# Two-layer RWKV-7 and differential-attention step: another deal of pair 9's matmuls, earlier loads in pair 0, and a group of outputs turned by VectorE and DMA

## Chip, cores and metric

The kernel runs on one core of a Trainium2 chip. The time is device microseconds from start to end of one execution; it is taken several times, and the median counts. The engines are TensorE (PE; its weight loads are shown apart as PEld), VectorE (DVE), ScalarE (ACT), GpSimd (POOL) and SyncE (SP), which issues nearly all DMAs. Each works through its own queue in order, and semaphores make one wait for another.

## What is computed

A trunk of two layers runs over 512 prompt tokens and 32 sample tokens. Each layer has one input projection, a token mixer, four heads of attention over a memory of 256 rows, a SiLU gate and one output projection.

```python
def rwkv_layer(...):           # layer 0
    h = rmsnorm(x, norm_w)
    p, qm, gate = jnp.split(h @ w_in, [RW_PROJ, RW_PROJ + MEM_W], axis=-1)
    y_mix, S_T, last_row = rwkv_mixer(p, ...)      # 24 heads of 64, a state update for each token
    y_mem = mem_attention(qm, mk, mv)
    out = jnp.concatenate([y_mix.astype(x.dtype), y_mem], axis=-1) * jax.nn.silu(gate)
    return x + out @ w_out, S_T, last_row

def diff_layer(...):           # layer 1
    attn = probs(q1, k1) - lam * probs(q2, k2)     # 12 heads, masked by chunks of 64
    o = einsum('bhqk,bkhd->bqhd', attn, v_all)
    o = rmsnorm(o, subln) * (1.0 - lam_init)
    out = jnp.concatenate([o, y_mem], axis=-1) * jax.nn.silu(gate)
    return x + out @ w_out, k, v
```

The memory's keys and values, the mixer's last state, and layer 1's keys and values are outputs as well.

## The kernel before

All large products are made of matmuls of 128x128 weights by 272 tokens, each operand split into a high and a low part, three matmuls a product (`ps_g<-hh,whi`, `hl,whi`, `hh,wlo`). They are the filling of the program: a stream hands out one at a time, and everything else is placed between them. A block of 48 such matmuls makes 128 columns of a projection; its weights come by DMA as `raw` and are split by ACT (`whi`) and DVE or POOL (`wlo`) one block ahead.

**Layer 0** does the 24 mixer heads as 12 pairs. For a pair `pr` the loop at L1540 runs through `PLAN`, 23 steps of two halves. At each step it issues one piece of the pair's chain over eight chunks of tokens (`go("chain", pr)`, three steps a chunk), then the plan's pieces of later pairs: `prep` two pairs ahead, which ends with the pair's chunk matrices in `at` and stores their diagonal blocks to DRAM (`sc<-at`, step 11, first half); `inv`, which loads them in another layout (`m<-sc`) and inverts them on POOL; `back`, which stores the inverse (`sc<-u`, step 9); `at` (L802), five DMAs that load it into `at` (`at<-sc`, `ats<-sc`, step 11, second half); and `mrg`, which from step 16 puts the inverse together with 32x32 matmuls, the first of which reads a DVE transpose of it (`t1b`, `ps_w<-t1b,at`). After each half it hands out filling matmuls until the planned time `t` reaches the half's due time. `each[pr]` counts the pair's filling matmuls: 130 for pair 0, 192 for pairs 1 to 8, 10 and 11, and 144 for pair 9. Due times (L1546) are spread over the steps by `pace` (L1545): evenly, or by each step's DVE load where the pair has fewer than 144. The DMAs go out on SP in program order, and one that waits holds up all behind it.

**Layer 1** is one stream of 2688 positions, a position being one filling matmul. Each of the 12 heads has three blocks (values, keys, queries), gates, and for heads 1, 3, 5 and 7 the query and gate of a memory head; head 5, the sixth, starts at position 1152 and has 288. Work is set on positions relative to a head's start `f`: at 52 the values are turned and later stored, at 99 and 108 the keys are split, exchanged by DMA (`kh<-kh`) and stored (`scr<-sg`); scores come at 156, 188, 220 and 254 (`ps_s`, then exponentials on ACT), and the normalized weights of each tile are turned by DVE in 32x32 blocks into `pk`. At 304 `pk` is stored by four DMAs (`ptr<-pk`), at 360 loaded back as `aT`, and at 440 multiplied with the values (`ps_o`), with the result scaled into `ot`. Four heads are a group.

At the end of a group, `norms` (L2080) makes the norm of its outputs, `scaled` (L2085) applies it to one head's `ot` and `finished` (L2099) turns it so that the model dimension lies on the partitions and multiplies it by the gate. There are two ways to turn it, chosen by `OTURN`, the number of groups that go the second way. In the first, four PE transposes write `ps_oT`. In the second, `spread` (L1792) transposes 32x32 blocks on DVE into `to` and four DMAs put the blocks of 128-byte rows in their places in DRAM (`spread<-to`); a DMA loads the result (`turned_back`). `to` has one buffer, which the memory heads' probabilities (`mspread<-to`) and the cached keys (`to<-ck`) use too. With `OTURN = 0` all three groups go the first way. The first group's norms stand at `begin(5) + NORM1` and its `finished` at positions 106, 130, 154 and 178 of head 5.

A memory head of layer 1 (`mem_steps`, L1134) is a generator of 14 pieces, set on positions by `MEMAT1`, for the last one, in head 7, by `MEMAT1B`: loads, scores and weights of two tiles each, three turns by `spread` (pieces 8, 11 and 12), the loads of the turned weights (13), and the product with the values (14, `ps_mo`). Head 8 starts 240 positions after head 7.

Of the kernel before, what the change touches and what calls it, by code (L numbers as in the profile page):

```python
# [19 lines left out]
KT = D // P  # L20
# [17 lines left out]
MEM1 = (1, 3, 5, 7)  # L38
TILES1 = ((156,178),(188,210),(220,244),(254,280))
MEMAT1 = (60, 80, 180, 276, 294, 306, 324, 330, 346, 362, 402, 420, 484, 552)  # L40
MEMAT1B = MEMAT1[:10] + (400, 430, 490, 590)
LOADS1, SPLITS1 = (1, 26), (4, 10, 14, 20)
SAMPLE1 = ((310, "s"), (338, "m"), (362, "t"), (386, "w"), (406, "n"), (464, "r"))
SAMPLE2 = ((186, "s"), (214, "m"), (228, "t"), (264, "w"), (311, "n"), (336, "r"))
TILES2 = ((152, 180), (210, 236), (240, 268), (272, 304))
BACK1, SUMS1, NORM1 = 80, 160, 52
BACK2, SUMS2, NORM2 = 54, 112, 34
SUMS3 = 22
NORM1B = 76
OTURN = 0  # L50
MTURN = True
CTURN = True
STEP, GAP1, GAP2 = 60, 70, 112
LATE = (186, 222, 254, 290)
OUT1 = 24
RKV = 4
# [13 lines left out]
PLAN = [  # L70
    [[("val", 0, 0.95, 0), ("prep", 2, 0.1, 0)], [("prep", 2, 0, 0.42)]],
    [[], [("prep", 2, 0, 1.04)]],
    [[("prep", 1, 0.53, 0)], [("prep", 1, 0, 0), ("prep", 2, 0.56, 1.0)]],
    [[("prep", 2, 0, 0)], [("prep", 2, 0, 1.0)]],
    [[("smp", 0, 0.11, 0.28), ("prep", 1, 0.4, 0)], [("prep", 2, 0, 0.86)]],
    [[("out", -1, 0.11, 0)], [("prep", 2, 0, 0.84)]],
    [[("prep", 2, 0, 1.1), ("smp", 0, 0.21, 0.29)], [("prep", 2, 0, 0.86)]],
    [[("prep", 2, 1.1, 1.37)], []],
# [52 lines left out]
class Trunk:  # L131
# [1219 lines left out]
    def layer0(self, mem):  # L1351
# [6 lines left out]
        with ExitStack() as ctx:  # L1358
# [24 lines left out]
            def go(kind, pr):  # L1383

                if kind == "rsq":
                    self.rsqrt(self.r20[:], self.q20[:], self.rk0, "nt20")
                elif 0 <= pr < NPAIR:
                    if kind in ("inv", "back", "at"):
                        {"inv": self.rw_invert, "back": self.rw_back, "at": self.rw_at}[kind](sts[pr])
                        return  # L1390
                    if (kind, pr) not in run:
                        it = run[kind, pr] = self.rw_prep(sts[pr], rkv[pr]) if kind == "prep" else make[kind](sts[pr])
                        next(it)
                    next(run[kind, pr], None)


            blocks, each = [], [0] * NPAIR
# [95 lines left out]
            def shift_out():  # L1493

                ps = self.psm.tile([P, 512], F32, tag="m", name="ps_sh")
                so = self.ma.tile([NPROJ, 2, P], F32, name="sho")
                for q in range(2):
                    self.te.transpose(ps[:NPROJ, q * P : q * P + P], self.shc[:, q, :], self.ident[:])
                self.ae.copy(so[:], ps[:NPROJ, :256].rearrange("p (q c) -> p q c", q=2))
                for q, n in ((0, 3), (1, 9)):  # L1500
                    self.se.dma_start(o[n][0, 0].rearrange("(j p) -> j p", p=P), so[:, q, :])
# [37 lines left out]
            for pr in range(NPAIR):  # L1539
                mplan = MPLAN.get(pr, ())  # L1540
                took = [HOP + sum(us for x in y for kind, d, us, _ in x if 0 <= pr + d < NPAIR) for y in PLAN]
                load = [HOPV[k % 3] + sum(us for x in y for kind, d, _, us in x if 0 <= pr + d < NPAIR) for k, y in enumerate(PLAN)]
                whole = sum(took) + MEMPE * len(mplan) / 12 + MAIN * each[pr]

                pace = [max(x, 1.4) for x in load] if each[pr] < 3 * 6 * KT else [1.0] * len(PLAN)  # L1545
                due = [whole * sum(pace[:k]) / sum(pace) for k in range(len(PLAN) + 1)]  # L1546
                room = (sum(load) + 2.3 * each[pr] / 48) / len(PLAN)
                t, left, spent = 0.0, each[pr], 0.0
                for k, y in enumerate(PLAN):
                    go("chain", pr)  # L1550
                    t += HOP
                    if (pr, k) == SHIFT_OUT:
                        shift_out()
                    spent += HOPV[k % 3]
                    for half, x in enumerate(y):
                        for kind, d, us, vus in x:
                            if 0 <= pr + d < NPAIR and kind != "full":
                                go(kind, pr + d)
                                t += us
                                spent += vus  # L1560
                        for at, h in mplan:
                            if at == k + half / 2:
                                if h not in mit:
                                    mit[h] = self.mem_steps(mems[h], 0, h, self.ma)
                                    next(mit[h])
                                next(mit[h], None)
                                t += MEMPE / 12
                        if k + half / 2 in EPLAN.get(pr, ()):
                            next(early)
                        if FULL not in x:  # L1570
                            spent += self.some(room * (k + (half + 1) / 2) + 0.4 - spent)
                        while left and t + MAIN / 2 < (due[k + 1] if half else (due[k] + due[k + 1]) / 2):
                            next(main)
                            t += MAIN
                            left -= 1
                while left:
                    next(main)
                    left -= 1
                if pr + 3 == NPAIR:
                    for _ in range(3):  # L1580
                        go("prep", pr + 2)
                    while self.later:
                        self.later.pop(0)[0]()
                    ca.close()
                    early = self.early_tiles(self.pool("wo0e", 1, ctx=mctx, side="right"), made)
                    self.ma = self.pool("mem0a", 1, ctx=ma, side="right")
# [10 lines left out]
        with ExitStack() as ctx:  # L1597
# [49 lines left out]
            pr = [self.psc.tile([P, 512], F32, tag="c", name="ps_r") for _ in range(2)]  # L1647
# [169 lines left out]
    def diff_layer(self, dq, p, mp, mctx, pool_early, order, made):  # L1817
# [7 lines left out]
        def at(pos, fn):  # L1825
            ev.append((pos, len(ev), fn))
# [45 lines left out]
        def make_query(ms):  # L1872
            def make(w):
                ms["q"], evac = self.query_evac(mp)
                yield from self.steps(w, lambda ps, v: evac(ps, v) and None)
            return make

        def make_mem_gate(ms, m):
            def make(w):
                _, ms["gate"], evac = self.gate_evac(self.o1[12 + m])  # L1880
                yield from self.steps(w, evac)
            return make
# [202 lines left out]
        def scaled(G, j):  # L2085
            ot = G["on"][j]
            self.ve.tensor_tensor(ot[:], ot[:], G["ss"][:, 2, 4 * j : 4 * j + 4].unsqueeze(2).to_broadcast([P, 4, P]), ALU.mult)
# [11 lines left out]
        def finished(G, hg, j):  # L2099
            if hg < OTURN:  # L2100
                x = G.pop(("oT", j))[:].rearrange("p t q -> p (t q)")
            else:
                ps = self.psm.tile([P, 512], F32, tag="m", name="ps_oT")
                for t in range(4):
                    self.te.transpose(ps[:, t * P : t * P + P], G["on"][j][:, t, :], self.ident[:])
                x = ps[:]
            g = self.o1[4 * hg + j]
            self.ve.scalar_tensor_tensor(g[:, :TP], x, self.subs, g[:, :TP], ALU.mult, ALU.mult)
            self.ve.tensor_tensor(g[:, TP:], G["oT"][:, 32 * j : 32 * j + 32], g[:, TP:], ALU.mult)
# [12 lines left out]
        for h, st in enumerate(sts):  # L2122
# [24 lines left out]
            if h in MEM1:  # L2147
                m = MEM1.index(h)
                makes += [make_query(mems[m]), make_mem_gate(mems[m], m)]
                for off in MEMAT1B if h == MEM1[-1] else MEMAT1:  # L2150
                    at(f + off, lambda m=m: next(mits[m], None))
            if h % 4 == 3:
# [5 lines left out]
                for j in range(4):  # L2158
                    if hg >= OTURN and not last:
                        at(b + 18 + 14 * j, lambda G=G, j=j: scaled(G, j))  # L2160
# [131 lines left out]
```

## Time and profile before

| | |
|---|---|
| median of 3 runs | 1372.35 us (1371.68 to 1373.49) |
| the profiled execution | 1371.31 us, of which 1369.6 us are span |
| mean granted TensorE clock | 0.991 |
| layer 0's pairs, first chain piece of each | 140 to 598 us, about 45.6 us apart |
| layer 1's stream | 826 to about 1260 us |

Rows of the timeline have the start and the length in us, the engine (SPq is SP's DMA queue), the operation, what it writes and reads (out<-in), its shape and its count, and in brackets how long the engine was idle before it and what released it. Rows of the waits have the engine and what it writes, what it waited for, and the sum, the number and the longest of these waits. A window's row has its stretch and length, the busy us and instructions of PE, PEld, DVE, ACT and POOL, the granted clock, the share of the DMA engines and GB/s.

### The profile page before, as it was taken

The page shows a single profiled execution, that of the slowest core. Times are in us where ns is not written, and L with a number is a line of the kernel's source. Part 1 is how long each engine was busy: PE and PEld are TensorE (multiplying, and loading weights), DVE is VectorE, ACT ScalarE, POOL GpSimd, SP SyncE. Part 2 cuts the span into 40 slices and gives each one's busy share as a digit, 9 for nine tenths or more (in the row PEclk, how much of TensorE's full clock was granted, in tenths as well). Part 3 has the DMA queues.
Part 4 walks back from the last instruction along what each step waited for, and adds up shares of the span by engine and source line. Part 5 has one row for each costly group of instructions (what it writes and reads, how often), then busy time and mean ns, then how long its engine had stood idle before and what let it go on. Part 6 is the DMA issues. An engine that isn't in the chain of part 4 may idle for free. (4 is left out here: it accounts for less than half of the span.)

```text
span 1369.6 us, 31286 instructions
## 1 busy us (share of the span) xinstructions
PE 1324.5 (97%) x11600; PEld 1268.7 (93%) x11600; DVE 888.7 (65%) x2203; ACT 771.8 (56%) x2090; POOL 562.0 (41%) x986
## 2 busy tenths in 40 slices
PE   6999999999999999999999999999999999999997
PEld 6998899999999999888899999999999999999997
DVE  6766667877787778756673374545675556767443
ACT  6665767677767776655652354545444454554321
POOL 1317675568556855560130034444333343542000
PEclk9999999999999999999999999999999999999998
DMA  7643223322332233233364456767676758784721
GB/s 230 185 118 76 62 67 86 86 74 63 86 86 74 63 86 77 74 84 99 99 206 128 133 154 180 179 143 181 143 174 146 171 134 179 169 190 145 241 70 66
DMA packets 418291, 171.47 MB, mean 125 GB/s; under 512 B 195210, under 2 KB 402579, under 8 KB 418139
## 3 DMA queue, kind: packets, MB, share of 16 engines
q1 hardware_dynamic: 417994, 168.96, 47.7%
q8 instruction: 91, 1.49, 0.5%
q14 instruction: 62, 0.50, 0.1%
q10 hardware_dynamic: 144, 0.52, 0.1%
HBM read 130.84 MB, written 41.92 MB: 126 GB/s over the span
## 5 line engine op out<-in xcount | busy, mean ns | idle before, releaser
L128 PE MATMUL ps_g<-hl,whi 128*128 128x272 f32 x1872 | 544.9, 294 | 0.6 <-POOL hl L500 0.5
L128 PE MATMUL ps_g<-hh,wlo 128*128 128x272 f32 x1808 | 538.7, 298 | 1.3 <-DVE wlo L128 1.3
L128 PE MATMUL ps_g<-hh,whi 128*128 128x272 f32 x1808 | 537.4, 297 | 0.9 <-ACT hh L128 0.9
L128 PEld LDWEIGHTS ps_g<-hl,whi 128*128 128x128 f32 x1872 | 353.7, 190 | 2.8 <-POOL hl L500 0.7
L128 PEld LDWEIGHTS ps_g<-hh,whi 128*128 128x128 f32 x1808 | 344.3, 190 | 5.3 <-ACT hh L128 1.3
L128 PEld LDWEIGHTS ps_g<-hh,wlo 128*128 128x128 f32 x1808 | 343.7, 190 | 5.8 <-DVE wlo L128 2.1
L128 ACT CAST whi<-raw 128x512 fp32r<-128x512 f32 x322 | 190.8, 617 | 95.1 <-PE ps_g L128 51.0
L789 POOL TENSOR_TENSOR tm<-u,m 102x84 f32<-102x84 f32 (+23 forms) x372 | 156.7, 421 | 165.8 <-DMA m<-sc 137.8
L338 POOL TENSOR_TENSOR wlo<-raw,whi 128x512 fp32r<-128x512 f32 x110 | 142.0, 1308 | 185.3 <-ACT whi L128 166.7
L128 DVE TENSOR_TENSOR wlo<-raw,whi 128x512 fp32r<-128x512 f32 x212 | 153.5, 739 | 74.5 <-ACT whi L128 73.1
L791 POOL TENSOR_TENSOR u<-u,tm 102x84 f32<-102x84 f32 (+23 forms) x372 | 159.0, 427 | 29.1
L128 PE MATMUL ps_g<-lo,whi 128*128 128x272 f32 x448 | 129.5, 289 | 0.7 <-DVE lo L128 0.7
L128 PE MATMUL ps_g<-hi,wlo 128*128 128x272 f32 x448 | 129.5, 289 | 0.2 <-DVE wlo L128 0.2
L128 PE MATMUL ps_g<-hi,whi 128*128 128x272 f32 x448 | 129.5, 289 | 0.1
L128 PEld LDWEIGHTS ps_g<-lo,whi 128*128 128x128 f32 x448 | 84.4, 188 | 1.1 <-DVE lo L128 1.1
L128 PEld LDWEIGHTS ps_g<-hi,wlo 128*128 128x128 f32 x448 | 84.5, 189 | 0.4 <-DVE wlo L128 0.4
L128 PEld LDWEIGHTS ps_g<-hi,whi 128*128 128x128 f32 x448 | 84.5, 189 | 0.3 <-ACT whi L128 0.3
L128 DVE SCALAR_TENSOR_TENSOR SB<-ps_c,dl,sd 64x64 f32<-64x64 f32 x168 | 47.3, 282 | 43.5 <-PE ps_c L128 39.3
L128 ACT COPY sv<-ps_c 64x64 f32<-64x64 f32 x192 | 39.2, 204 | 38.9 <-PE ps_c L128 37.1
L1890 POOL TENSOR_TENSOR kz<-k,kh 64x544 fp32r<-64x544 f32 x24 | 33.4, 1392 | 53.3 <-ACT kh L128 52.4
L1660 POOL TENSOR_TENSOR hl<-hn,hh 128x544 fp32r<-128x544 f32 x8 | 12.4, 1557 | 92.6 <-ACT hh L128 92.5
L128 ACT ACTIVATE qp<-ps_g 64x272 fp32r<-64x272 f32 x48 | 18.8, 391 | 50.6 <-DVE qp L128 33.7
(395 smaller groups left out, 2560.9 us busy)
## 6 DMA issues: line engine op xcount, KB each, us to landing
raw<-in_rw_in_dram SPq DMA_DIRECT2D x114, 256.0 KB
raw<-in_df_in_dram SPq DMA_DIRECT2D x112, 256.0 KB
raw<-in_w_out_dram SPq DMA_DIRECT2D x64, 256.0 KB
ptr<-pk SPq DMA_DIRECT2D x44, 160.0 KB
aT<-ptr SPq DMA_DIRECT2D x11, 640.0 KB
scr<-sg SPq DMA_DIRECT2D x96, 68.0 KB
out_dram<-scr SPq DMA_DIRECT2D x6, 1024.0 KB
m<-sc SPq DMA_DIRECT2D x36, 128.0 KB
```

Of the source, the lines that this page charges most:

```text
L128: return lambda *a, **k: self.trunk.tie(self, issue(*a, **k))
L338: todo.append((lambda k=k, q=q: low.tensor_tensor(lo[:, k], raw[q][:], hi[:, k].bitcast(F32), ALU.subtract), LATER))
L789: nc.gpsimd.tensor_tensor(tm[:, :n, :wd], u3[:, :n, kx : kx + 1].to_broadcast(sh), m3[:, kx : kx + 1, kx + 1 :].to_broadcast(sh), ALU.mult)
L791: nc.gpsimd.tensor_tensor(u3[:, :n, kx + 1 :], u3[:, :n, kx + 1 :], tm[:, :n, :wd], ALU.add)
L1660: nc.gpsimd.tensor_tensor(self.hl[:, k, :], h[:], self.hh[:, k, :].bitcast(F32), ALU.subtract)
L1890: nc.gpsimd.tensor_tensor(self.kz[h % 2][rows[m], m, :], k[rows[m], :], hi.bitcast(F32), ALU.subtract)
```

## The change

Three things are changed.

1. In layer 0 the due times of a pair with exactly 144 filling matmuls, which is pair 9, are spread by load instead of evenly.
2. In pair 0 the five loads of pair 1's inverse are issued at the start of step 11, right behind the chain's piece, instead of in its second half behind `prep`'s five stores of pair 2. The other pairs keep the order.
3. In layer 1 `OTURN` is 1: the first group's four heads are turned by DVE and DMA. Their norms move from position 52 to 94 of head 5; head j is scaled and turned at 112 + 50 j, stored at 122 + 50 j, loaded at 182 + 50 j and finished at 224 + 50 j. The memory head in head 7 has its pieces 8 to 14 at 356, 366, 382, 406, 436, 496 and 596 instead of 330, 346, 362, 400, 430, 490 and 590.

```diff
-MEMAT1B = MEMAT1[:10] + (400, 430, 490, 590)
+MEMAT1B = MEMAT1[:7] + (356, 366, 382, 406, 436, 496, 596)
...
-BACK1, SUMS1, NORM1 = 80, 160, 52
+BACK1, SUMS1, NORM1 = 80, 160, 94
...
-OTURN = 0
+OTURN = 1
...
-STEP, GAP1, GAP2 = 60, 70, 112
+STEP, GAP1, GAP2 = 50, 70, 112
...
-                pace = [max(x, 1.4) for x in load] if each[pr] < 3 * 6 * KT else [1.0] * len(PLAN)
+                pace = [max(x, 1.4) for x in load] if each[pr] <= 3 * 6 * KT else [1.0] * len(PLAN)
...
                     spent += HOPV[k % 3]
+                    if (pr, k) == (0, 11):
+                        go("at", 1)
                     for half, x in enumerate(y):
                         for kind, d, us, vus in x:
+                            if (pr, kind) == (0, "at"):
+                                continue
                             if 0 <= pr + d < NPAIR and kind != "full":
```

The code of the second way is there already:

```python
                        x = b + 18 + STEP * j
                        at(x, lambda G=G, j=j: (scaled(G, j), turned_out(G, j)))
                        at(x + 10, lambda G=G, j=j: turned_stored(G, j))
                        at(x + GAP1, lambda G=G, j=j: turned_back(G, j))
                        at(x + GAP2, lambda G=G, hg=hg, j=j: finished(G, hg, j))
```

## The prediction

> **What bounds the kernel now.** I read the page first, then who TensorE (PE) waited for, then stage windows.
>
> ```profile
> span 1369.6 us, 31286 instructions
> PE 1324.5 (97%) x11600; PEld 1268.7 (93%) x11600; DVE 888.7 (65%) x2203; ACT 771.8 (56%) x2090; POOL 562.0 (41%) x986
> ...
> 160.00:180.00 20.00, 17.69 (x162) 16.22 (x163) 11.20 (x36) 12.10 (x35) 6.47 (x24) 0.83 0.38 90
> 1022.00:1030.00 8.00, 8.00 (x68) 8.00 (x67) 5.10 (x13) 3.40 (x11) 5.05 (x4) 1.00 0.85 139
> 1030.00:1050.00 20.00, 20.00 (x157) 19.71 (x156) 12.60 (x36) 9.73 (x28) 5.08 (x4) 1.00 0.54 148
> 551.50:597.10 45.60, 40.63 (x413) 37.45 (x408) 32.06 (x79) 27.46 (x83) 29.80 (x75) 0.96 0.25 63
> 186.00:551.50 365.50, 362.10 (x3688) 342.62 (x3689) 288.33 (x719) 269.57 (x774) 233.19 (x515) 1.00 0.30 77
> ```
>
> PE is busy in 97% of the span, and the windows (length, then busy us of PE, weight loads, DVE, ACT, POOL, then granted clock, DMA share, GB/s) say where it isn't. Pairs 1 to 8 (186 to 551.5 us) leave it 3.4 us idle in 365; the sixth head of layer 1 (1022 to 1050) nothing. Pair 9 leaves 5.0 us in 45.6, and 160 to 180, in pair 0, 2.3 us, with the clock at 0.83 besides. So a change pays in two ways: it fills one of these holes, or it takes work off PE where PE is full. All sums are against the profiled execution (1371.31 us, of which 1369.6 are span); the median of the three runs shown, 1372.35, lies 1.04 above it, and the forecast is set against that median.
>
> **The loads of pair 1's inverse, moved (pair 0).**
>
> ```profile
> 163.39 2.13 SPq L128 DMA_DIRECT2D sc<-u  x6
> 165.62 2.73 SPq L128 DMA_DIRECT2D sc<-at  x4
> ...
> 168.94 1.86 SPq L128 DMA_DIRECT2D at<-sc  x4
> ...
> 171.39 2.04 SPq L128 DMA_DIRECT2D m<-sc  x6
> ...
> 170.02 0.17 DVE L128 TENSOR_SCALAR q<-ps_ss 128x10 f32<-128x10 f32 x1 [1.17 <-PE ps_ss L128]
> 170.71 0.43 DVE L128 STREAM_TRANSPOSE t1b<-at 32x256 f32<-32x256 f32 x1 [0.52 <-DMA at<-sc]
> 171.90 0.43 DVE L128 STREAM_TRANSPOSE t1b<-at 32x256 f32<-32x256 f32 x1 [0.76 <-DMA at<-sc]
> ...
> PE ps_w L128 <- DVE t1b L128: 1.4, 2, 0.9
> ...
> 89.31 0.38 SPq L128 DMA_DIRECT2D sc<-ats  x1
> ...
> 90.92 2.02 SPq L128 DMA_DIRECT2D m<-sc  x6
> ```
>
> The queue of SP stores the inverse (sc<-u), then pair 2's blocks (sc<-at, sc<-ats), and only then loads pair 1's inverse back; the DVE transposes t1b wait for those loads, and PE for t1b, 1.4 us in two waits (167 to 175). The edit puts the five loads ahead of the five stores of pair 2. They can't start until the six stores have landed; 89.69 to 90.92 bounds a landing at 1.2 us behind the last issue, so they go at 165.52 + 1.2 = 166.7 instead of 168.94, 2.2 us sooner. Then t1b waits for its turn instead: behind q it ends at 170.2 + 2 x 0.43 = 171.1 instead of 172.33. **Term: -1.2 us**, between 0 (the landing is as slow as the queue was) and -1.4 (both waits).
>
> What is late next: pair 2's five stores start behind the loads, at 169.1, land at some 173.5, and m<-sc, which feeds the inversion on POOL, goes at 173.5 instead of 171.39. So the inversion ends 2.1 us later than before.
>
> ```profile
> 205.90 3.17 SPq L128 DMA_DIRECT2D sc<-u  x6
> ...
> 210.20 1.96 SPq L128 DMA_DIRECT2D sc<-at  x4
> ...
> 212.76 1.86 SPq L128 DMA_DIRECT2D at<-sc  x4
> ...
> 217.61 0.90 DVE L128 STREAM_TRANSPOSE t1b<-at 32x256 f32<-32x256 f32 x2
> ```
>
> In pair 1 sc<-u then goes at 208.0 and the loads behind it still at about 212.8, since sc<-at isn't issued before 210.2 there anyway; the third load, issued at 213.7, lands 2 us later (that of pair 0, issued at 169.9 as the third of four, released t1b at 171.90), at 215.7, and t1b, 1.2 us sooner, wants it at about 216.8. The cover is 1 us; were it gone, at most the 1.2 us would be lost.
>
> **The deal of pair 9.** Its 144 filling matmuls (0.12 us each, by the window from 1022 to 1030: 68 matmuls in 8.00 us of a full PE) are dealt by load instead of evenly. Working the plan's table through, the count ahead of step 3 falls from 15 to 13, ahead of step 7 rises from 50 to 54, ahead of step 14 from 90 to 95; at the end both are 144. Nothing is added.
>
> ```profile
> 556.42 0.49 PE L128 MATMUL ps_c<-avz,at 128*128 128x128 f32 x2 [1.04 <-DVE avz L128]
> 564.25 1.16 PE L128 MATMUL ps_at<-zr,bk 64*128 64x128 f32 x16 [0.68 <-DVE bk L128]
> 577.81 0.39 PE L128 MATMUL ps_g<-hh,wlo 128*128 128x272 f32 x1 [0.68 <-DVE wlo L128]
> 582.48 0.24 PE L128 MATMUL ps_w<-t1b,at 32*32 32x32 f32 x2 [0.92 <-DVE t1b L128]
> ```
>
> The wait at 556.42 (step 3) grows by the two matmuls taken away, 0.24. Between it and 564.25 (step 7) lie 41 matmuls instead of 35: 0.72 us, enough for the 0.68. The wait at 577.81 falls on the third matmul of a weight block, number 99, which now comes five matmuls sooner in step 14; the split is forced at the block's start, so it moves up too, and I take no gain. At 582.48 (step 16) two more matmuls lie ahead, 0.24. Sum 0.68 - 0.24 + 0.24 = 0.7 where DVE doesn't move; since part of what PE does sooner must wait for DVE again, I take **-0.5**, between -1.6 (the 0.68, 0.68 and 0.24 all gained) and +0.8 (the seven matmuls dealt forward leave a later wait bare).
>
> **The first group's outputs off PE.**
>
> ```profile
> 1018.43 0.29 PE L128 MATMUL ps_g<-hh,whi 128*128 128x272 f32 x1
> 1018.55 0.60 PE L128 MATMUL ps_oT<-ident,ot 128*128 128x128 f32 x4
> ...
> 1019.12 0.29 PE L128 MATMUL ps_g<-hh,wlo 128*128 128x272 f32 x1
> ...
> L128 DVE STREAM_TRANSPOSE to<-ck x3: 704/704/716, 852.3 to 1153.9; 128x512 f32<-128x512 f32 x3
> ...
>   DMA mspread<-to: 18.4, 5
> ...
> 1022.91 3.88 SPq L128 DMA_DIRECT2D ptr<-pk  x4
> ...
> 990.35 2.74 SPq L128 DMA_DIRECT2D mspread<-to  x4
> ...
> 996.28 0.45 DVE L128 STREAM_TRANSPOSE to<-mp 128x256 f32<-128x256 f32 x1 [2.03 <-DMA mspread<-to]
> 1029.96 0.75 DVE L128 SCALAR_TENSOR_TENSOR og<-ps_oT,dv,og 128x512 f32<-128x512 f32 x1 [0.83 <-PE ps_oT L128]
> ...
> PE ps_s L128 <- ACT pt L128: 1.2, 2, 0.7
> ...
> PE ps_s L128 <- DMA kh<-kh: 1.1, 2, 0.6
> PE ps_mo L128 <- DVE og L128: 0.7, 1, 0.7
> PE ps_s L128 <- ACT pt L128: 0.4, 1, 0.4
> ```
>
> Removed: 16 transposes, four at a time. From 1018.43 to 1019.12 is 0.69 us for one four and two filling matmuls (0.24): 0.45 each four, 1.8 us in all, and PE is full there. Added: four DVE transposes of 0.70, 16 stores (2.74 us of SP for four) and four loads. SP and the DMA engines have room behind 1030 (share 0.54), and the weights they bring are loaded more than a block of 48 positions ahead, so I cost the queueing at nothing; were that cover gone, a store's 2.74 us would stand in front of a weight load. The norms move with it, by 42 positions: some ten small DVE operations now lie ahead of the keys' turn instead of behind the last head's scores, off PE's path as long as the keys' own copy on ACT feeds PE. The closing products stay on DVE, and read SBUF instead of PSUM. The new wait is on DVE: all turns share one buffer, to, so a turn waits until the stores of the one before have landed, 996.28 - 990.35 = 5.9 us from the first issue; behind it queue the maxima of the next score tile, the gates' second halves, and through the exponentials PE's next score tile.
>
> The sixth head's positions take about 0.16 us: the first ps_oT (position 106) starts at 1018.55, the last (178) is done when DVE goes on at 1029.96, 72 positions in 11.4 us. Turn 0's stores follow the keys' and ptr, which end at 1026.8, and land at 1032.7; turn 1 (position 162, 56 behind the first ps_oT) is due at 1027.5: a wait of 5.2. Turn 2 and 3, 8 us on each: 3.8 and 2.5. In all 11.5 us of DVE waiting. What such a wait costs PE: the five of before, 18.4 us, go with PE waits at the score tiles (ps_s for ACT pt) of 1.2 us from 840 to 1105 and 0.4 from 1105 to 1185: 1.6 us, 9%. So 1.0. **Term: -1.8 + 1.0 = -0.8**, between -1.8 and +2.2 (what doesn't fit DVE's idle time: 11.5 + 2.8 against 10.3 idle from 1022 to 1050, 4.0 less 1.8).
>
> The Trainium skill (VectorE: DVE Perf Modes, "Rules for kernel authors") speaks against this part: a 128x128 transpose belongs on TensorE where its result may lie in PSUM, as it may here. By that rule the work should stay, and the term would be a loss; by the rows above PE is what is full, so the dearer path is cheaper as long as DVE's wait stays hidden.
>
> **The eighth head's memory steps, up to 26 positions later.**
>
> ```profile
> 1134.24 2.45 SPq L128 DMA_DIRECT2D mspread<-to  x4
> ...
> 1137.32 1.12 SPq L128 DMA_DIRECT2D kh<-kh  x2
> ```
>
> The four stores at 1134.24 now come behind the ninth head's keys, so kh<-kh goes 2.5 us sooner and PE's wait of 1.1 us for it ends (the rows from 1105 to 1185 above). But SP is full until the second turn's stores, which come no sooner, and DVE waits for them as before: I let the wait for ACT pt (0.4) grow by the 1.1. The last step, six matmuls later, arrives 0.7 us later and covers the 0.7 of ps_mo; I take 0.5 of it. **Term: -0.5**, between -2.2 (all three rows) and +0.5 (the first turn's stores, now behind the keys', hold up DVE's second turn by the 0.5 gained).
>
> **Sum:** -1.2 - 0.5 - 0.8 - 0.5 = -3.0: 1368.3 for the profiled execution, **1369.3** against the median.
>
> **Rivals.**
>
> *Half clock shortened* (0.12). 160 to 180 has a granted clock of 0.83: 3.4 us lost. If the merge's filling matmuls come 1.2 us sooner, the slow stretch could end one step earlier, half of it: 1.7 more, 1367.6. For it: matmuls replace the wait. Against: the wait is 1.4 us of those 20, and the merge's own 32x32 matmuls stay as thin as they are. The Trainium skill (TensorE: Matmul & The Clock Gate, "What you observe") says half clock lasts until one window of about 3.4 us is busy, and that the window runs free; the trace agrees in size, and by the rule this could fall either way from run to run.
>
> *Saved PE time lands in the next wait* (0.31). DVE sets the end of heads 6 and 9, so those terms are given back, and pair 9 gains half: -1.2 - 0.3, 1370.9. For it: DVE's wait of 5.2 in a stretch that had none. Against: 9% in the past.
>
> *The deal hurts* (0.08): +0.9 instead of -0.5, 1370.7.
>
> *Slower* (0.13): the added stores slow their own landing. In the sixth head DVE's waits already use up its idle time; each further us of landing counts three times on PE. At 2 us more (7.9 instead of 5.9) PE loses 4.0 + 6 us, less 1.8 and 2.2: +6.0, 1378.4. It becomes a loss of over 0.2% from about 6.8 us of landing on. For it: DMA share 0.85 up to 1030. Against: 0.54 after.
>
> Forecast: 0.36, its own range 1367.5 to 1371. A measurement tells about 0.2% (2.7 us) from no change: the limit is 1369.6, so the forecast and the clock rival give faster 0.44; the given-back cases and the forecast's upper part same 0.43; slower 0.13. The range reaches from the clock rival with a little more to the edge of the slower case: 1366.3 to 1373.
>
> **What would show it.** at<-sc behind sc<-u, and t1b of pair 0 without a DMA wait, for the first term; PE's waits for bk and wlo in pair 9 for the second; 32 instead of 48 ps_oT, DVE's waits on spread<-to, and PE's waits at the sixth head's score tiles for the third; kh<-kh gone from PE's waits, and what stands at ps_s and ps_mo after it, for the fourth. The forecast is wrong if PE's idle time from 1022 to 1050 exceeds 1.8 us, or if pair 1's t1b waits for its loads.

## The result, and the profile after

| | median | runs |
|---|---|---|
| kernel before, measured beside it | 1370.35 us (1367.35 to 1374.56) | 14 |
| changed kernel | 1375.33 us (1372.87 to 1379.89) | 14 |

The ratio is 1.0039, with a 95% interval from 1.0029 to 1.0048: slower by 0.39%, 5.3 us by the ratio, where 3.0 us less were forecast. The profiled execution of the changed kernel took 1376.06 us. First its page, then its windows (columns as in the prediction; a packet counts in the window in which it starts, so that the share of the DMA engines can pass 1 in a short one):

```profile
span 1374.3 us, 31289 instructions
...
PE 1325.4 (96%) x11584; PEld 1270.2 (92%) x11584; DVE 894.9 (65%) x2207; ACT 772.5 (56%) x2090; POOL 565.0 (41%) x986
```
```profile
553.00:599.00 46.00, 42.23 (x459) 38.60 (x454) 32.53 (x83) 30.08 (x89) 29.46 (x73) 1.00 0.29 77
1022.00:1050.00 28.00, 27.05 (x211) 26.54 (x210) 19.01 (x46) 11.33 (x33) 11.18 (x9) 1.00 0.77 171
...
1068.79:1073.79 5.00, 3.87 (x34) 3.69 (x33) 0.44 (x1) 0.42 (x2) 0.47 (x1) 1.00 1.20 267
1073.79:1078.79 5.00, 4.13 (x33) 3.91 (x32) 1.81 (x4) 0.88 (x3) 0.00 (x0) 1.00 0.63 120
1078.79:1083.79 5.00, 3.22 (x17) 3.22 (x18) 4.02 (x16) 3.18 (x11) 2.51 (x2) 0.77 0.50 140
```

The 16 transposes are gone from PE, and its busy time still grew by 0.9 us: matmuls take longer at half clock (0.43 us a filling matmul at 1082, 0.29 at 1081), and the mean granted clock of this execution is 0.989, that of the kernel before 0.991. Pair 9 leaves PE idle for 3.8 us instead of 5.0. The sixth head (1022 to 1050) leaves it idle for 0.95 us: the forecast put 1.0 there. The loss stands behind it. In the **seventh head**, where the prediction looked at nothing, PE is idle for 1.1, 0.9 and 1.8 us in three windows of 5 us each, and the last of them has a granted clock of 0.77. Counted from each head's first filling matmul to the next head's, the seventh head took 33.0 us instead of 28.95.

Who waited there, in the views of the waits (engine and what it writes, what it waited for, sum, times, longest) of the changed kernel, PE from 1048 to 1090 and DVE from 1020 to 1085:

```profile
PE ps_s L128 <- ACT pt L128: 2.7, 1, 2.7
PE ps_o L128 <- DMA aT<-ptr: 1.1, 1, 1.1
...
DVE to L128 <- DMA mspread<-to: 7.2, 1, 7.2
DVE to L128 <- DMA spread<-to: 5.8, 2, 3.8
DVE og L128 <- DMA oTt<-spread: 3.9, 1, 3.9
...
```

The kernel before has no wait of PE over 0.13 us there. The new waits on DVE in the sixth head (5.8 us in two for `to`) are half the 11.5 that the prediction counted. Two others stand in the seventh: 3.9 us for the fourth head's load `oTt`, and 7.2 instead of 5.4 for the memory's stores. The queue of SP there, in the timelines (start, length), first before and then after:

```profile
1050.30 3.26 SPq L128 DMA_DIRECT2D ptr<-pk  x4
...
1055.61 1.92 SPq L128 DMA_DIRECT2D mspread<-to  x4
...
1063.63 1.58 SPq L128 DMA_DIRECT2D kh<-kh  x2
...
1067.91 2.81 SPq L128 DMA_DIRECT2D mspread<-to  x4
```
```profile
1053.36 3.98 SPq L128 DMA_DIRECT2D ptr<-pk  x4
...
1058.65 2.51 SPq L128 DMA_DIRECT2D mspread<-to  x4
1061.21 0.50 SPq L128 DMA_DIRECT2D oTt<-spread  x1
...
1067.52 1.76 SPq L128 DMA_DIRECT2D kh<-kh  x2
...
1071.74 2.94 SPq L128 DMA_DIRECT2D mspread<-to  x4
```

Both heads begin at nearly the same time (1048.97 and 1048.79). `ptr` starts 3.1 us later, because the turn `pk` that it stores is late on DVE; the second `mspread` starts 3.8 us later. Behind it come the memory's third turn on DVE, which needs the buffer `to`, and PE's score tile. DVE before and after:

```profile
1049.56 0.71 DVE L128 STREAM_TRANSPOSE pk<-pt 128x512 f32<-128x512 f32 x1
...
1072.73 0.45 DVE L128 STREAM_TRANSPOSE to<-mp 128x256 f32<-128x256 f32 x1 [5.43 <-DMA mspread<-to]
```
```profile
1052.62 0.71 DVE L128 STREAM_TRANSPOSE pk<-pt 128x512 f32<-128x512 f32 x1
...
1064.59 0.82 DVE L128 SCALAR_TENSOR_TENSOR og<-oTt,dv,og 128x512 f32<-128x512 f32 x1 [3.92 <-DMA oTt<-spread]
...
1076.46 0.45 DVE L128 STREAM_TRANSPOSE to<-mp 128x256 f32<-128x256 f32 x1 [7.16 <-DMA mspread<-to]
```

And how full the DMA engines were in the first 25 us of this head, before and after (the view of DMA):

```profile
DMA packets 17998, 4.01 MB, mean 160 GB/s; under 512 B 14017, under 2 KB 17869, under 8 KB 17997
...
q1 hardware_dynamic: 17997, 3.99, 79.8%
```
```profile
DMA packets 19590, 4.80 MB, mean 192 GB/s; under 512 B 14084, under 2 KB 19460, under 8 KB 19588
...
q1 hardware_dynamic: 19588, 4.77, 90.6%
```

The share of 0.54 on which the prediction rested ends at 1050. Right behind it the engines were busy for 80% of 25 us already, and the change made it 91%. The Trainium skill (DMA: Bandwidth & Descriptors, "Specifications") puts the least size for full rate at 512 bytes. The trace agrees: in the changed kernel's 25 us the 14084 packets under 512 bytes, nearly all of 128, move 151 GB/s in the time in which they keep the engines busy, and the 5506 larger ones, nearly all of 512, move 272. That the engines are this full is shown; whether it is what costs the time is asked below.

### The profile page after: what moved, and what is told of

It is laid out like the page before. It is cut to its first block, busy times and chain, and to the rows that moved or that the text cites. A ratio compares the mean times of both kernels' runs of the same rounds, so it can differ in the third digit from the quotient of the medians.

```text
span 1374.3 us, 31289 instructions
## 1 busy us (share of the span) xinstructions
PE 1325.4 (96%) x11584; PEld 1270.2 (92%) x11584; DVE 894.9 (65%) x2207; ACT 772.5 (56%) x2090; POOL 565.0 (41%) x986
## 5 line engine op out<-in xcount | busy, mean ns | idle before, releaser
L128 ACT COPY sv<-ps_c 64x64 f32<-64x64 f32 x192 | 39.4, 205 | 41.2 <-PE ps_c L128 39.4
L128 ACT ACTIVATE pt<-ps_s,snm 128x128 f32<-128x128 f32 (+3 forms) x48 | 25.3, 527 | 39.7 <-DVE snm L128 39.3
```

The source lines that it names most:

```text
L128: return lambda *a, **k: self.trunk.tie(self, issue(*a, **k))
```

## The experiments

All kernels below are the kernel before plus the edit shown; all ratios are against the kernel before, measured on the same chip in five rounds.

### The four parts one by one

`e1_at`: only the diff's lines on `"at"`.

> Only the moved loads of pair 1's inverse. Theory (the loss sits in the seventh head of layer 1, and pair 0's gain is given back in pair 1): PE's wait for t1b in pair 0 gone, pair 0 shorter by 1 to 2 us; in pair 1 a new PE wait of about 1.4 us (ps_q for POOL's rkk), since POOL's inversion ends 1.5 us later; time against before -0.4 us, between -1 and +0.6 (ratio 0.9993 to 1.0004). Rival A (the move is what costs: POOL's later inversion reaches further pairs): +2 us or more, ratio 1.0015 or above. Rival B (the term as predicted): -1.2 us, ratio 0.9991, and no wait in pair 1.

Measured: 1372.41 us against 1369.13, ratio 1.0018 (1.0005 to 1.0032). Neither expectation of a small change held; the time is rival A's. Its reason isn't in the rows: pairs 2 to 8 together take 320.3 us, and 318.3 to 320.8 in the executions without this edit (half of the time at half clock taken off). The wait that the theory named is there, with 0.7 us instead of 1.4. The whole change has the same edit; its timelines of SP, DVE and PE are these, and last PE's row in e1:

```profile
162.75 2.13 SPq L128 DMA_DIRECT2D sc<-u  x6
165.86 1.78 SPq L128 DMA_DIRECT2D at<-sc  x4
...
172.85 2.00 SPq L128 DMA_DIRECT2D m<-sc  x6
```
```profile
171.33 0.90 DVE L128 STREAM_TRANSPOSE t1b<-at 32x256 f32<-32x256 f32 x2
```
```profile
208.71 0.73 PE L128 MATMUL ps_q<-rkk,hb 128*128 128x272 f32 x2 [1.36 <-POOL rkk L714]
```
```profile
207.87 0.73 PE L128 MATMUL ps_q<-rkk,hb 128*128 128x272 f32 x2 [0.73 <-POOL rkk L714]
```

The loads go right behind the stores, `t1b` waits for no DMA, and PE's wait for it falls from 1.4 us to 0.2. Yet no gain is to be seen: ten of the sixteen profiled executions in this document leave these loads where they were, and in eight of them PE waits for `t1b` there for 0.2 us or not at all; only the kernel before (1.4) and e9 (0.8) show the wait. And `m<-sc` goes at 172.85 instead of 171.39 (2.1 us later, counted from `sc<-u`), and in pair 1 of the changed kernel PE waits 1.36 us for `rkk`, a product of pair 3's preparation that the kernel queues on POOL (`spare`, L684). POOL's timeline before and after:

```profile
203.43 1.35 POOL L714 TENSOR_TENSOR rkk<-rkv 128x544 f32<-128x544 f32 x1
...
205.64 0.23 POOL L791 TENSOR_TENSOR u<-u,tm 102x11 f32<-102x11 f32 x1
```
```profile
207.14 0.23 POOL L791 TENSOR_TENSOR u<-u,tm 102x11 f32<-102x11 f32 x1
207.32 1.34 POOL L714 TENSOR_TENSOR rkk<-rkv 128x544 f32<-128x544 f32 x1
```

Before, `rkk` stood ahead of the inversion's last two rounds; now it stands behind them. The edit touches no POOL instruction, and yet their order changed; the traces show that, not why. So `rkk` starts 3.9 us later, while the inversion's end moved by 1.5. Pair 1, from its first chain piece to the next pair's, takes 46.0 to 46.5 us in the ten executions without the edit, 47.1 in e1 and 47.8 in the changed kernel.

`e2_deal`: only `<` to `<=` in L1545.

> Only the deal of pair 9 by load. Theory: pair 9 shorter by 0.5 us beside any change of the half clock there (with it up to 2.2), PE's waits for bk and t1b gone, those for avz up by 0.25; ratio 0.9996, between 0.9985 and 1.0001. Rival (the seven matmuls dealt forward leave a later wait bare, or the next stretch begins thinner): +0.8 us, ratio 1.0006.

Measured: 1368.35 against 1369.13, 0.9989 (0.9978 to 1.0001). The waits of the changed kernel in pair 9, from 552 to 599, are those of this run too, to 0.1 us:

```profile
PE ps_c L128 <- DVE avz L128: 1.3, 1, 1.3
PE ps_v L128 <- ACT sv L128: 0.9, 1, 0.9
PE ps_y L128 <- DVE yt L128: 0.4, 1, 0.4
PE ps_g L128 <- DVE wlo L128: 0.4, 1, 0.4
...
```

The waits for `bk` and `t1b` are gone, that for `wlo` fell from 0.68 to 0.38, and that for `avz` grew from 1.04 to 1.3 as worked out. (The one for `yt` isn't new: most executions without the deal have 0.2 to 0.3 there.) In all PE idles 1.2 us less.

`e3_oturn`: only `OTURN = 1`, `NORM1 = 94`, `STEP = 50`.

> Only the first group's outputs by VectorE's blocks and DMA, with their new places. Theory: nearly the whole loss is here. Sixth head shorter by about 1 us; seventh head longer by about 4 us and the eighth by about 1 (half clock behind the stall): DVE waits 3.9 us there for the fourth load oTt, which SP issued only after ptr, a weight block and mspread; behind it the keys' turn, the second memory turn and, through the one buffer to, PE's score tile wait of 2.6 us. Time +4.3 us, ratio 1.0031 (1.0020 to 1.0040). Rival A (landing slowed by the added stores, in the sixth head): same total, but PE's idle time lies between 1022 and 1050. Rival B (the parts only lose together, or the memory steps lose): -0.8 to +1 us, ratio below 1.0008.

Measured: 1373.17 against 1369.13, 1.0026 (1.0016 to 1.0036): most of the loss, and in the seventh head (33.3 us long), as the theory had it.

`e4_mem`: only the new `MEMAT1B`.

> Only the eighth head's memory steps, later. Theory: PE's waits for kh (1.1 us) and ps_mo (0.7) go, and waits at the score tiles (ps_s for ACT pt, 1.2 us more) and for the next head's keys (about 1.2 us) take their place: 0 us, between -0.8 and +0.6 (ratio 0.9994 to 1.0004). Rival A (the memory steps are where the time is lost): +2 us or more, ratio 1.0015. Rival B (the term as predicted): -0.5 us, 0.9996 - told from the theory only by the rows, not by the time.

Measured: 1370.07 against 1369.13, 1.0006 (0.9995 to 1.0016): not to be told from nothing. In the changed kernel, the waits of PE from 1108 to 1200:

```profile
PE ps_s L128 <- ACT pt L128: 1.6, 1, 1.6
PE ps_s L128 <- DMA kh<-kh: 1.2, 1, 1.2
```

The waits for the ninth head's keys and `ps_mo` went. The one for `pt` grew from 0.4 to 1.6, and one for the tenth head's keys is new (1.7 in e4 itself): the four loads `mpT` now stand close ahead of them on SP, at 1168.59 with the keys at 1173.23. That these loads are what delays the keys was not tried by itself.

The four ratios add up to +0.39%, as much as the whole change. Each is uncertain by 0.1%, so this shows no disturbance between the parts, but it couldn't show a small one.

### Why the outputs cost time

The first theory: DVE's wait for the fourth load holds up the keys' turn and the memory's second turn. `e5_late3` takes DVE's wait away, `e9_load63` puts the load ahead of `mspread`, `e10_norm52` puts everything 42 positions earlier. `e6_at_dve` went with them, on the moved loads.

```diff
e5   at(x + GAP2 + 60 * (j == 3), lambda G=G, hg=hg, j=j: finished(G, hg, j))
e9   at(x + GAP1 - 7 * (j == 3), lambda G=G, j=j: turned_back(G, j))
e10  BACK1, SUMS1, NORM1 = 80, 160, 52
e6   (e1 and)  spare = nc.gpsimd if pr > 3 else self.ve
```

> The first group's outputs alone, as in e3, but the closing products of the fourth head 60 positions later (some 9.6 us), behind the seventh head's second memory turn. Theory (a DVE instruction that waits for a late load holds the keys' turn and, through the buffer to, PE's score tile): DVE's wait of 5.0 us for oTt and PE's of 2.5 us for ACT pt go, and the half clock behind it (1.7 us); PE's 0.9 us for aT stays and some 0.8 us of a score tile wait; time against before +0.9 us, ratio 1.0007 (0.9996 to 1.0015), 2.5 to 4 us under e3. Rival A (the loss is the load on SP's queue, 20 more DMA issues, whatever DVE waits for): as e3, ratio 1.0020 to 1.0030, with PE's stall at another tile of the seventh head. Rival B (as predicted once this wait is gone): -0.8 us, 0.9994.

> The first group's outputs alone, as in e3, but the fourth head's load oTt seven positions earlier, ahead of the memory's stores mspread on SP's queue instead of behind them; nothing else is moved. Theory: the load goes 2.7 us sooner, DVE's wait for it falls from 5.0 to about 2.3 us, PE's wait at the score tile from 2.5 to about 1 us, and the half clock behind it may go: ratio 1.0012 (1.0003 to 1.0024), between e5 and e3. Rival A (the number of DMA issues, not their order, is what costs): as e3, 1.0026.

> The first group's outputs alone, as in e3, but all of it 42 positions (some 6.7 us) earlier, the norms ahead of the sixth head's keys as in the kernel before. Theory: the fourth load is issued ahead of ptr and the memory's stores, DVE doesn't wait for it in the seventh head, and PE's waits there go: -0.3 us, ratio 0.9998 (0.9988 to 1.0008). Rival A (stores ahead of the keys' on SP's queue, so that the sixth head's keys come late): PE waits for kh or aT in the sixth head, ratio 1.0008 to 1.0030. Rival B (the turned outputs cost the same wherever they stand): 1.0020 to 1.0032.

> The moved loads alone, as in e1, with pair 3's product r*k2 on DVE instead of POOL. Theory (the move reordered POOL's queue: the inversion starts later and the product fell behind its last four steps, and PE waits for it in pair 1): the wait for rkk goes, and the gain of pair 0 is left: -0.8 us against before, ratio 0.9994 (0.9984 to 1.0003), clearly under e1's 1.0018. Rival A (e1's loss lies elsewhere, since its profiled run shows only 0.7 us there): as e1, 1.0012 to 1.0024. Rival B (DVE pays for the product, 0.7 us in front of the chain of pair 1): in between, 1.0002 to 1.0010.

Measured: e5 1.0036 (1.0023 to 1.0050), e9 1.0027 (1.0017 to 1.0036), e10 1.0063 (1.0049 to 1.0078), e6 0.9996 (0.9986 to 1.0006). **The first theory fell**: in e5 DVE doesn't wait for the load in the seventh head at all, in e9 2.6 us instead of 5.0, and PE loses as much as in e3 or more. Here is e5's memory turn and, behind it, the closing product, in DVE's timeline:

```profile
1076.39 0.45 DVE L128 STREAM_TRANSPOSE to<-mp 128x256 f32<-128x256 f32 x1 [8.90 <-DMA mspread<-to]
...
1078.24 0.75 DVE L128 SCALAR_TENSOR_TENSOR og<-oTt,dv,og 128x512 f32<-128x512 f32 x1
```

What DVE doesn't wait for the load it waits longer for the memory's stores (8.9 us). The stores are what is late. For e6 the theory held in what concerns the loss: without POOL's `rkk` the wait in pair 1 is gone, and the pair takes 46.1 us again, as in the executions without the moved loads. The gain of pair 0 that it left over isn't to be seen, neither in e6's interval nor in the pair.

e10 lost more than any of its expectations allowed. Half of the loss lies in the sixth head, for which only its rival A expected a wait, and another one: it takes 52.3 us, where eight executions with PE's transposes take 47.5. The third turn waits for the buffer `to`, and PE behind it at a score tile (DVE, then PE):

```profile
1033.21 0.71 DVE L128 STREAM_TRANSPOSE to<-ot 128x512 f32<-128x512 f32 x1 [5.80 <-DMA spread<-to]
```
```profile
1036.97 0.44 PE L128 MATMUL ps_s<-kh,qp 128*128 128x384 f32 x1 [4.22 <-ACT pt L128]
```

This is the wait that the prediction priced at 9% of DVE's; here 6.5 us of DVE's waiting for these stores go with 4.2 us of PE's.

The second theory: from `ptr` to the second `mspread` SP's queue is one chain without slack. `e11_split` clears it, `e12_dma` puts only transfers into it, and `e15_dve` only makes it start late.

```diff
e11 (e3 and)
-                        x = b + 18 + STEP * j
-                        at(x, lambda G=G, j=j: (scaled(G, j), turned_out(G, j)))
+                        x = b + 18 + (0, STEP, 341, 391)[j]
+                        at(b + 18 + STEP * j, lambda G=G, j=j: scaled(G, j))
+                        at(x, lambda G=G, j=j: turned_out(G, j))
e12 (at head 6)
+                for off, part in ((-16, "store"), (-6, "load"), (44, "load")):
+                    at(f + off, lambda part=part: extra(part))
e15 (at head 6, position f - 10)
+                    for _ in range(7):
+                        self.ve.scalar_tensor_tensor(x[:], y, 1.0, y, ALU.mult, ALU.mult)
```

> The first group's outputs alone, as in e3, but the turns of the third and fourth head with their stores, loads and closing products come behind the seventh head's memory turns (291 positions later, some 46 us); the scaling stays. e5 and e9 took DVE's wait for oTt away or halved it and PE lost as much, so that theory fell. New theory (the stretch of SP's queue from ptr to the memory's second stores is a chain with no slack: in all of e3, e5, e9 and e10 it starts 2.2 to 2.9 us late and carries the output's stores or loads through full DMA engines, so that the memory's third turn comes 3.1 to 4.4 us later after the head's start than before): with the stretch free, PE's waits for aT and pt in the seventh head go, and PE's saved work is left; -0.9 us against before, ratio 0.9993 (0.9983 to 1.0004). Rival A (the turned outputs cost their loss wherever they stand, through DVE's and SP's time): 1.0015 to 1.0030.

> The kernel before, with what the outputs put on SP and the DMA engines at the start of the seventh head and nothing on DVE: four stores of 32x512 (128-byte rows) where the fourth turn's stand, and two transfers of 128x512 (512-byte rows) where the third and the fourth load stand, of a tile that is only read. Theory A (the transfers' load lengthens the stretch): ptr starts as before, the memory's second stores 1 to 2 us later than 18.9 us after the head's start, PE waits 1 to 2 us at the score tile; ratio 1.0010 (1.0003 to 1.0024). Theory B (only the late start of ptr counts, the added transfers find room): as before, 0.9996 to 1.0004.

> The kernel before, with seven DVE products of 128x128 (about 0.3 us each, some 2.2 us) ahead of the sixth head's last score tile's normalization, and no transfer added. Theory B (late start: the last turn pk of the sixth head comes 2 us later, ptr and all behind it too, and the DMA engines are too full to catch up): the memory's third turn 2 us later, PE waits about 2 us at the seventh head's score tile, sometimes with 1.7 us of half clock behind it; ratio 1.0016 (1.0007 to 1.0028). Theory A (only the added transfers count, a late start is made up): 0.9997 to 1.0005.

Measured: e11 0.9994 (0.9983 to 1.0004), e12 1.0009 (1.0000 to 1.0018), e15 1.0023 (1.0014 to 1.0033). e11 and e15 came out as the theory had them, save that PE's wait for `pt` in e11 fell to 1.31 us and did not go; e12 can't be told from either of its two theories. The timeline of e15, DVE and SP, shows a late start at work with no transfer added:

```profile
1048.14 2.24 DVE L128 SCALAR_TENSOR_TENSOR dmy<-hh 128x128 f32<-128x128 f32 x7
...
1051.59 0.71 DVE L128 STREAM_TRANSPOSE pk<-pt 128x512 f32<-128x512 f32 x1
```
```profile
1052.33 3.27 SPq L128 DMA_DIRECT2D ptr<-pk  x4
...
1069.84 2.82 SPq L128 DMA_DIRECT2D mspread<-to  x4
```

The kernels in one table, in us after the seventh head's first filling matmul, from the timelines of the profiled executions:

| | `pk` starts | `ptr` | second `mspread` | third turn `to` | PE waits (`ps_o` for aT, `ps_s` for pt) |
|---|---|---|---|---|---|
| before | 0.59 | 1.33 | 18.94 | 23.76 | -, 0.13 |
| e1, e2, e4, e6, e13: this head as before | 0.59 | 1.33 | 18.39 to 19.52 | 23.14 to 24.21 | -, 0 to 0.59 |
| e12, transfers only | 0.59 | 1.33 | 19.53 | 24.34 | -, 0.71 |
| e11, split | 2.94 | 3.68 | 20.24 | 24.94 | -, 1.31 |
| e15, DVE only | 2.75 | 3.49 | 21.00 | 25.53 | -, 1.90 |
| e10, earlier | 0.59 | 3.48 | 22.26 | 26.88 | 0.38, 2.63 |
| e5, late product | 3.51 | 4.25 | 22.43 | 27.23 | 0.67, 3.58 |
| e3, outputs | 3.00 | 3.74 | 22.78 | 27.32 | 0.89, 2.54 |
| changed kernel | 3.83 | 4.57 | 22.95 | 27.67 | 1.13, 2.65 |
| e9, earlier load | 3.42 | 4.16 | 23.67 | 28.19 | 1.62, 2.71 |

PE's wait is the third turn less 23.63, to 0.01 us, as long as it is the only one; from e10 on a second wait stands ahead of it, and the two together come to 3.0 to 4.3. So the head of the kernel before had nothing to give: PE waits 0.13 us for its third turn already. And this turn moves by 1.1 us between executions that leave the head alone (second row), so that smaller differences say nothing. Measured against that:

- A late start costs by itself. `pk` 2.16 us late makes the third turn 1.8 later in e15, with no transfer added. Elsewhere less of it arrives: 1.2 of 2.35 us in e11, and 0.1 of 1.3 in e14, a version further down.
- What stands in the queue costs as well. e3 and e11 have `pk` at the same place (3.00 and 2.94), and e3's third turn comes 2.4 us later. Its `aT` keeps PE waiting too, for 0.89 us, and e11's doesn't. e3 has the fourth turn's stores, two loads and two closing products there, and e11 has not. e5 moved one of the products and e9 one of the loads and gained nothing; which of the rest counts is open.
- The added transfers alone (e12) can't be told from nothing: its third turn at 24.34 is within 0.13 us of e13's, where the head is as before. Its stores went 7 us ahead of the head, since no DVE work held them back, so it weighs mainly the load behind `mspread`.

That the fullness of the DMA engines is the reason is therefore not shown. That a `pk` as late as e15's and the additions of e3 reach PE through this chain is. e10 shows another way into the same queue: `pk` is on time, but the load `oTt` ahead of `ptr` waits for its one buffer, and SP waits with it.

### Versions made of the parts

`e13_best` is e2 and e6 together; `e14_all` adds e11 to it and puts the second head's closing product 60 positions later; `e17_mem` is the whole change with e6's and e11's edits.

```diff
e14  at(x + GAP2 + 60 * (j == 1), lambda G=G, hg=hg, j=j: finished(G, hg, j))
```

> The two parts that gained, without the others: the deal of pair 9, and the moved loads with pair 3's product r*k2 on DVE. Theory (they lie in different pairs and add up, -1.5 from the deal and -0.5 from the loads): -2.0 us, ratio 0.9985 (0.9975 to 0.9996). Rival (the gains are the scatter of the half clock, and don't add up): 0.9993 to 1.0004.

> The deal, the moved loads with pair 3's product on DVE, and the first group's outputs split as in e11, with the second head's closing products 60 positions later; the memory steps as before. Theory (the gains are those of PE's rows and add up: 1.2 in pair 9, 0.8 in pair 0, 0.5 in the sixth head, and the seventh head's 1.3 us wait of e11 shrinks to under 0.7, since the last turn of the sixth head comes about 1 us sooner): -2.2 us, ratio 0.9984 (0.9974 to 0.9996). Rival (as e13 had it, the single gains were partly scatter): 0.9990 to 1.0002.

> As e14 without the moved closing product, and with the eighth head's memory steps moved as in the change: the whole change with its two queue costs taken out. Theory: the seventh head's wait is 1.3 us as in e11, the memory steps are worth nothing (their waits for kh and ps_mo only change their names): -1.2 us, ratio 0.9991 (0.9981 to 1.0002), 5 to 6 us under the changed kernel. Rival (the memory steps cost 1 us beside outputs that now end in the eighth head): 0.9998 to 1.0010.

Measured: e13 0.9998 (0.9989 to 1.0007), e14 0.9985 (0.9975 to 0.9996), e17 1.0000 (0.9989 to 1.0011). e14 is **faster than both kernels** (1368.20 against 1369.40). In its rows pair 9 is 1.3 us shorter than the mean without the deal and the sixth head 0.5, and its seventh head is back among those left alone: `pk` at 1.90, the third turn at 23.86, PE's wait 0.24. e17 takes the whole 0.39% back from the change with one edit of order and one product on another engine; its ratio lies in the range of its theory and in that of its rival. Against e14 it is 0.15% longer, about what the two intervals leave open, and the memory steps and the closing product can't be separated in it. e13 went against its expectation, though its rows in pair 9 are those of e2.

## Why the prediction was wrong, step by step

| part | forecast | alone | mended | its stretch in the profiled executions, without and with the part |
|---|---|---|---|---|
| loads of pair 0 | -1.2 | +2.5 | -0.5 (e6) | pair 0: 38.2 to 39.5, 39.1 to 39.2; pair 1: 46.0 to 46.5, 47.1 and 47.8 (46.0 to 46.2 with `rkk` on DVE) |
| deal of pair 9 | -0.5 | -1.5 | | pair 9: 42.0 to 43.0, 41.2 to 41.4 |
| first group's outputs | -0.8 | +3.6 | -0.8 (e11) | sixth head: 47.5, 46.7 (e3); seventh: 28.6 to 29.4, 33.3 (e3) |
| memory steps | -0.5 | +0.8 | | ninth head: 32.3 to 35.9, 32.1; tenth: 22.5 to 23.9, 24.4 to 26.3 |

(us. Forecast, alone and mended are differences, the last two the ratios of the runs by 1369 or 1370, each uncertain by 1.4 to 1.9 us on either side, so that the mended values can't be told from nothing. The last column has lengths, from a pair's first chain piece or a head's first filling matmul to the next one's. Half of the time at half clock is taken off those of the pairs, not of the heads.)

**The step that failed** is this one: "SP and the DMA engines have room behind 1030 (share 0.54), and the weights they bring are loaded more than a block of 48 positions ahead, so I cost the queueing at nothing". The share was read up to 1050, and the fourth head's stores and the last two loads fall at 1049.16 and behind it, into 25 us with 80%. What was priced as a danger to weight loads was one to `ptr`, `aT`, the keys and the memory's stores. In the place of nothing the runs showed 4.05 us in the seventh head of the changed kernel (33.0 instead of 28.95), from a `pk` 3.2 us late and the stores, loads and closing products behind it. The order on SP's queue, issue by issue, to the end of the last load would have shown it.

**The waits in the sixth head**: a loss of 1.0 on PE was forecast there, and 0.95 is in the windows. The agreement is luck: it was 9% of 11.5 us of DVE's waiting, and DVE waited 5.8 us; in e10 6.5 us of it cost 4.2. The head itself did get shorter, by 0.5 us in the changed kernel and 0.8 in e3. But from the last of these waits, at 1040.27, to `pk` at 1052.62 DVE has no wait, with the added scalings, turns and closing products among its work. They make `pk` 3.2 us late at the head's end, which costs nothing there and is paid for in the next head. The marker that was to show the forecast wrong, PE's idle time from 1022 to 1050, ended where the loss begins; the other one, a wait of pair 1's `t1b`, did not come either.

**The loads of pair 0**: this term failed too. The move itself came out (`at<-sc` 2.2 us sooner was forecast; counted from `sc<-u`, 2.4 came), but the 1.2 us were read from one execution, and the wait that they stand on is 0.2 us or none in eight of the ten that leave the loads in place. Pair 0 is no shorter with the move. What was late next was looked for at `t1b` of pair 1 and found covered, and it was: no DMA wait is there. That the inversion on POOL ends 2.1 us later was in the working, and counted from `sc<-u` it did; what else stands on POOL's queue was not. e6 shows that this is what pair 1 loses, 0.9 us in e1 and 1.6 in the changed kernel, against the mean of 46.2 without the move. That leaves part of e1's 2.5 us open; its interval reaches down to 0.7.

**The deal** had the right direction and was priced too low, at 0.5 us: in five executions with it pair 9 takes 41.2 to 41.4 us, in eleven without it 42.0 to 43.0, 1.4 less in the mean. The wait for `t1b`, of which 0.24 was to go, went whole, and that for `wlo` fell by 0.3 where nothing was counted. e13's time doesn't show this gain, its pair 9 does (41.2). **The memory steps** came out in that the wait for `pt` takes the place of that for the keys; the next head's keys were missed, again on SP's queue. The ninth head gets shorter and the tenth longer; both together take 55.4 to 56.7 us without the part and 56.5 to 57.1 with it, half of the time at half clock taken off.

**The base** was high: the three runs gave 1372.35 us, the fourteen 1370.35.

**The rivals**: that half clock gets shorter from 160 to 180 can't be told from chance. The granted clock there is 0.83 in the kernel before and 0.91 in the changed one, but 0.91 in e3 and 1.00 in e2 as well, which leave pair 0 alone. (The sentence that the prediction takes from the Trainium skill, TensorE: Matmul & The Clock Gate, stands in its section "What's actually happening".) That the saved PE time lands in the next wait was nearest in kind, but it kept to the same head. The slower case had the right sign and the wrong place: it let the stores slow their own landing in the sixth head. The rule weighed beside the outputs (the Trainium skill, VectorE: DVE Perf Modes, "Rules for kernel authors": a 128x128 transpose belongs on TensorE) is neither borne out nor refuted: the same turns cost 0.26% in one place (e3), and in another (e11) nothing that can be measured.

## What to carry to other kernels

When a part moves work onto a queue, follow that queue to the last of its added issues and into the next stage, and look there for the chain with no slack; a mean share that ends where the stage ends says nothing about it. What is late at the end of a stage without a wait is still late, and the next stage pays. Before a wait of one profiled execution is priced, see whether a second execution has it. And look at the changed program's order on every engine, also on those that the edit doesn't touch.

## What was not expected of the hardware

SP's four issues of `ptr` took 3.20 to 3.29 us in before, e11, e12 and e15, and 3.96 to 4.43 in the changed kernel, e3, e5, e9 and e10, where an `oTt` load goes within 3 us ahead of them. So an issue on SP isn't a fixed price here; it was dearer where other transfers had just been started.

The granted clock falls to half in stretches of 3.4 us, or of two or three times that. In all sixteen profiled executions one begins between 134 and 137 us and one stands at the end; the others come at places that change. With mean granted clocks of 0.987 to 0.994 the executions lost 8.5 to 17.9 us of clock (the time at half clock, halved). The 35 runs of the kernel before that stand beside the first experiments went from 1366.19 to 1375.29 us; single profiles can't be compared by their spans, and a row of one profile only after a look at the same row in others: PE's wait for `t1b` in pair 0 went from none to 1.4 us with nothing changed there.
